# Windowed attention of an odd layer as one plan over 64 head groups, TensorE in source order

## The chip, the cores and the metric

The kernel runs on one core of a Trainium2 chip. The metric is the device time of one execution in microseconds. The five engines run side by side, each with its own queue in order: TensorE (PE; its weight loads are shown as PEld), VectorE (DVE), ScalarE (ACT), GpSimd (POOL) and SyncE (SP), which here only issues DMAs.

## The reference

Two layers over 2048 latent tokens of width 1024, with 256 context tokens beside them. The even layer (Fourier mixing beside latent attention with 8 heads) is not touched by the change. The odd layer is

```python
q, k, v, g = split_cols(h_lat @ w_in, ODD_SPLITS)      # 16 q heads, 4 kv heads, head width 64
ck, cv = split_cols(h_ctx @ w_in[:, GQA_Q:GQA_Q + 2 * GQA_KV], (GQA_KV, GQA_KV))
s_ctx  = einsum('bnqhgd,bchd->bnhgqc', qb, kc) * GQA_SCALE        # 256 context tokens
s_band = einsum('bnqhgd,bnkhd->bnhgqk', qb, kb) * GQA_SCALE       # 3 blocks of 128 tokens
s_band = where(abs(qpos - kpos) <= 128 and 0 <= kpos < n, s_band, -inf)
p = softmax(concatenate([s_ctx, s_band, s_sink], axis=-1))        # a sink logit per head
y_l = (windowed_gqa(q, k, v, ck, cv, sink_hg) * silu(g)) @ w_out
x = x + g_l * y_l;  out = rmsnorm(x, final_g)
```

All is in f32 with split operands: a number is a rounded high part plus the rest, and a product of two such is three matmuls.

## The kernel before

The last stage of the kernel works on 16 blocks of 128 query tokens. A block has four head groups (kv = 0 to 3), each of four q heads that share one k and v head. A group has 5 key tiles of 128 (two of context, three of the band; 4 in the first and the last block). So there are 64 groups and 312 steps; one step is one key tile of one group.

`step6` (L1809) does a step. On PE it computes the scores, transposed (keys by 4 x 128 queries), into a PSUM bank: a mask matmul at the band's two ends (L1813), the high parts' product with q's two halves stacked over 128 rows (L1814), and k's low part (L1815), whose extra rows carry the negated row maximum, so that the exponent's shift comes with the matmul. ACT takes the exponential twice, to f32 (L1819) and to f16 (L1820). The difference of the two is the low part `pl`; L1821 lets POOL compute it, and DVE in two of a block's twenty steps. The products with v (PV) are put in a list `pvq` and run four steps later: three f16 matmuls for each of four heads (L1831 to L1833, 65, 64 and 65 columns), which sum high and low parts of v into the same columns. They accumulate over a group's steps in one of two PSUM banks (`ppv`). At a group's end DVE divides by the sum plus the sink term (L1837 to L1840), and POOL multiplies by the gate (L1842).

The maximum of a query's scores is needed before its first step. So a block ahead, for each of 16 heads, the plain scores are computed again: `max_band` (L1525, reduced by DVE in L1529) and, two heads at a time, `max_ctx` (L1538, L1541). `chain` (L1545) combines the maxima of all 16 heads of the next block with small DVE operations, and `aug` (L1564) transposes them for a group on PE (L1566) and writes them under q's high part (L1567). `load_q6` (L1502) loads a group's q from DRAM by three DMAs, into one of six slots; `prep_k` (L1475) loads a key tile.

The output of the block before is woven in: `out_load` (x from DRAM), `out_tr` (eight PE transposes, L1868, split by ACT and DVE), `out_mm` (48 matmuls at L186 to L188, with one PSUM bank, `ppo`, for everything) and `out_fin` (L1885): the square sum on ACT, the power on POOL (L191), the multiply by scale and gain on DVE (L1894), and the store by SP. The output weights are loaded and split (`wload`, `wsplit`) during block 0.

For each block a plan is made: a list of (position in the block from 0 to 1, function), from the tables in `TP`. After every step the functions due by then are emitted, then PV down to four waiting ones; what is left of the plan comes at the block's end, `out_fin` last (0.999). SP's DMAs are held to the order of emission (L150). PE's instructions are not, in this stage: the scheduler that builds the program may exchange them. In the even layer's attention (main function `step`, matmuls at L155, L1188 on POOL) PE is held to the order of emission, tiles go by pairs, and PV is two matmuls a head with 129 and 65 columns.

Before this stage, the odd layer's projections run in 15 passes (n = 0 to 14); the lists `e6` are emitted between the matmuls of passes 11 to 14 and hold constants, the first key tiles, block 0's q, all maxima of block 0, its chain and the first `aug`.

## Time and profile before

| | us |
|---|---|
| median of 3 runs (lowest, highest) | 3039.12 (3033.49, 3039.51) |
| the profiled execution | 3034.24 |
| its span, first to last instruction | 3032.2 |
| PE busy in the span | 2861.0 |
| POOL, DVE, ACT busy | 1632.0, 1462.6, 1427.4 |
| mean granted clock of PE | 0.983 |

Busy time of PE is from the starts of its matmuls to modelled ends, so it is not PE at its peak. A view of waits names who ended an engine's idle time. A view of groups gives, for each line and shape, the count, the busy time, the mean of one and the idle time before. A timeline gives each instruction's start and length. DVE, ACT, POOL, PE and SP stand for the engines named above; sbf, sbr and sby are SBUF, psb is PSUM, q1h and q1l are q's two parts in DRAM.

### The profile page before, as it was taken

How to read it: one execution, taken by the hardware profiler on the slowest of the kernel's cores; microseconds unless marked ns; L12 is line 12 of the kernel's file. 1: busy time of each engine (PE TensorE's matmuls, PEld its weight loads, DVE VectorE, ACT ScalarE, POOL GpSimd, SP SyncE). 2: the span in 40 equal slices, each digit the busy share in tenths (PEclk: the TensorE clock that was granted, in tenths of full speed). 3: DMA queues.
4: the chain of work that ended last, by engine and by line, in shares of the span. 5: the costliest groups of instructions: out<-in, count | busy, mean ns of one | idle time of the engine just before them, and what ended most of it. 6: DMA issues, size and time to landing. Idle time of an engine off the chain costs nothing. (4 is left out here: it accounts for less than half of the span.)

```text
span 3032.2 us, 54284 instructions
## 1 busy us (share of the span) xinstructions
PE 2861.0 (94%) x21388; PEld 2299.7 (76%) x21388; DVE 1462.6 (48%) x2884; ACT 1427.4 (47%) x2131; POOL 1632.0 (54%) x1221
## 2 busy tenths in 40 slices
PE   7999999999999999999999998999997899999998
PEld 4787777877777777777777888989786666677666
DVE  3323315453656665666542234323234666676664
ACT  4333213223577777777773332232222645554554
POOL 2202204035588888888784434353443766766665
PEclk9999999999999999999999998999998999999999
DMA  6453335466310111011016545544464333223321
GB/s 240 153 177 134 130 122 173 142 213 223 104 44 26 44 40 44 26 44 40 26 35 232 188 153 177 187 141 162 152 189 156 105 105 98 84 77 93 102 83 45
DMA packets 299399, 357.13 MB, mean 118 GB/s; under 512 B 40884, under 2 KB 210172, under 8 KB 299144
## 3 DMA queue, kind: packets, MB, share of 16 engines
q1 hardware_dynamic: 231320, 258.73, 27.0%
q10 hardware_dynamic: 67824, 94.93, 8.9%
q8 instruction: 168, 2.75, 0.4%
q14 instruction: 87, 0.71, 0.1%
HBM read 245.82 MB, written 107.76 MB: 117 GB/s over the span
## 5 line engine op out<-in xcount | busy, mean ns | idle before, releaser
L186 PE MATMUL psb<-sbr 128*128 128x512 f32 (+3 forms) x2054 | 744.3, 363 | 14.4 <-ACT sbf L1022 5.7
L188 PE MATMUL psb<-sbr 128*128 128x512 f32 (+3 forms) x2054 | 722.9, 352 | 4.8 <-DVE sbr L183 4.8
L187 PE MATMUL psb<-sbr 128*128 128x512 f32 (+3 forms) x2054 | 723.8, 352 | 2.2 <-POOL sbr L183 2.2
L1188 POOL TENSOR_TENSOR sbf<-sbf 128x1024 f16<-128x1024 f32 (+1 forms) x296 | 624.2, 2112 | 140.8 <-ACT sbf L1187 76.9
L155 PE MATMUL psb<-sbr 100*128 100x512 f32 (+1 forms) x2408 | 624.2, 399 | 21.0 <-DVE sbr L955 14.4
L155 PEld LDWEIGHTS psb<-sbr 100*128 100x128 f32 (+1 forms) x2408 | 425.0, 190 | 112.8 <-issue 17.3
L942 DVE TENSOR_REDUCE sbf<-psb 128x1 f32<-128x512 f32 (+1 forms) x584 | 400.7, 690 | 218.1 <-PE psb L155 203.5
L186 PEld LDWEIGHTS psb<-sbr 128*128 128x128 f32 (+1 forms) x2054 | 390.7, 190 | 81.0 <-issue 12.3
L188 PEld LDWEIGHTS psb<-sbr 128*128 128x128 f32 (+1 forms) x2054 | 390.2, 190 | 63.9 <-DVE sbr L183 6.8
L187 PEld LDWEIGHTS psb<-sbr 128*128 128x128 f32 (+1 forms) x2054 | 390.8, 190 | 53.2 <-POOL sbr L183 3.9
L1821 POOL TENSOR_TENSOR sbf<-sbf 128x512 f16<-128x512 f32 x282 | 338.0, 1213 | 116.0 <-issue 60.1
L1186 ACT ACTIVATE sbf<-psb 128x1024 f32<-128x1024 f32 (+1 forms) x296 | 299.6, 1012 | 200.4 <-PE psb L155 180.5
L183 DVE TENSOR_TENSOR sbr<-sbf,sbr 128x512 fp32r<-128x512 f32 (+3 forms) x212 | 209.1, 1014 | 382.2 <-ACT sbr L180 381.1
L180 ACT CAST sbr<-sbf 128x512 fp32r<-128x512 f32 (+4 forms) x286 | 198.2, 731 | 394.5 <-PE psb L187 149.5
L183 POOL TENSOR_TENSOR sbr<-sbf,sbr 128x512 fp32r<-128x512 f32 (+4 forms) x113 | 166.1, 1482 | 367.9 <-ACT sbr L180 226.3
L1819 ACT ACTIVATE sbf<-psb 128x512 f32<-128x512 f32 x312 | 188.4, 604 | 282.1 <-PE psb L1815 249.8
L1187 ACT ACTIVATE sbf<-psb 128x1024 f16<-128x1024 f32 (+1 forms) x296 | 297.8, 1006 | 0.0
L155 PEld LDWEIGHTS <-sbf 128*128 128x128 f16 x4672 | 213.5, 97 | 72.9 <-issue 65.9
L155 PE MATMUL psb<-sbf 128*128 128x129 f16 (+1 forms) x4672 | 256.8, 207 | 5.2 <-DVE sbf L1214 2.9
L1529 DVE CUSTOM_DVE_ANT_0 sbf<-psb,sbf 128x384 bf16<-128x384 f32 (+1 forms) x256 | 137.8, 538 | 119.4 <-PE psb L1525 108.1
L1820 ACT ACTIVATE sbf<-psb 128x512 f16<-128x512 f32 x312 | 188.2, 603 | 5.5 <-DMA vd<-sbf 5.5
L1831 PEld LDWEIGHTS <-sbf 128*128 128x128 f16 x1248 | 115.5, 97 | 68.3 <-issue 61.8
(259 smaller groups left out, 4303.9 us busy)
## 6 DMA issues: line engine op xcount, KB each, us to landing
sbf<-in_o_w_in_t SPq DMA_DIRECT2D x60, 512.0 KB
sbf<-in_w_in_t SPq DMA_DIRECT2D x54, 512.0 KB
sbf<-in_x SPq DMA_DIRECT2D x32, 512.0 KB
sbf<-in_w_mod SPq DMA_DIRECT2D x32, 512.0 KB
sbr<-q1h SPq DMA_DIRECT2D x128, 128.0 KB
h1d<-sbf ACTq DMA_DIRECT2D x9, 1024.0 KB
sbf<-h1d SPq DMA_DIRECT2D x18, 512.0 KB
x1d<-sbf ACTq DMA_DIRECT2D x16, 512.0 KB
```

The lines of the kernel that those rows point to most:

```text
L155: tc.keep_in_program_order(nc.tensor.matmul(*args, **kw))
L180: act.copy(hi, src)
L183: e_lo.tensor_sub(lo, src, hi)
L186: pe.matmul(ps, sh, mh, start=start, stop=False)
L187: pe.matmul(ps, sh, ml, start=False, stop=False)
L188: pe.matmul(ps, sl, mh, start=False, stop=stop)
L942: dve.reduce_max(st["mx"][:, js[0] : js[-1] + 1, c], ps[:, 0 : len(js) * kn].rearrange("p (j k) -> p j k", k=kn), axis=AX.X)
L1186: act.activation(pf[:, :, 0:n], ps[:, :, 0:n], AF.Exp, scale=MLA_SCALE)
L1187: act.activation(ph[:, :, 0:n], ps[:, :, 0:n], AF.Exp, scale=MLA_SCALE)
L1188: pool.tensor_sub(pl[:, :, 0:n], pf[:, :, 0:n], ph[:, :, 0:n])
L1819: act.activation(pf, ps, AF.Exp, scale=GQA_SCALE)
L1821: (dve if (TP["b0"].get("sub", TP["sub"]) if b == 0 else TP["sub"])[kv][n] else pool).tensor_sub(pl, pf, ph)
```

## The change

The stage gets one plan for all 312 steps instead of one for each block, with positions counted in steps.

- PE is held to the order of emission in this stage too.
- Maxima, chain, sink and augment go by groups: a group's maxima lie 9 to 5 steps ahead of its first step, its chain (a DVE reduction over three values, a negation on ACT, an addition on POOL, the sink's exponential on ACT) right behind, its `aug` 2.2 steps ahead. The negated maximum is one rounded row set of 4, no longer a high and a low one (72 rows become 68).
- A group's q is loaded five groups ahead.
- Steps go by pairs: the f32 and f16 exponentials lie in two-tile buffers, and POOL subtracts 1024 columns at once. DVE subtracts only in the last group.
- PV is two matmuls a head with 129 and 65 columns; a group's sums take two PSUM banks, in one buffer instead of two. PV runs after every second step, down to six waiting ones; a group's last PV is moved ahead of the next step where it is first in the list.
- At a group's end DVE adds the low part by four scalar-tensor operations. The multiply by the final gain goes from DVE to POOL, the scaling of the output row to ACT.
- The two transposes of the output stand 3.2 steps apart, its matmuls 0.95 steps each, and `out_fin` follows 25 steps after the end of its own block.
- Block 0's maxima of the third and fourth group move out of the stage before; q and key tiles for block 0 are loaded a pass earlier there.

```diff
@@ tables of positions @@
-    'b0': {'mx': [0.1, 0.41, 0.59, 0.68], 'mcd': [0.1, 0.26, 0.08, 0.13]},
-    'pps': 3,
-    'ppv': 2,
-    'ppo': 1,
-    'ppx': 2,
-    'sub': [[0, 0, 0, 0, 1], [0, 0, 0, 0, 0], [0, 0, 1, 0, 0], [0, 0, 0, 0, 0]],
-    'lag': 4,
...
@@ const6 @@
+        C6["mask4"] = c6.tile([4, 4, P], F32, name="mask4b")
+        sp.dma_start(C6["mask4"], A["c_mask8"][0:4])
+        for u in range(8):
+            C6["mx", u] = c6.tile([P, 4, 3], F32, name=f"mx6{u}")
+            act.copy(C6["mx", u][:, :, 2], sk8[:, u % 4 * 4 : u % 4 * 4 + 4])
...
@@ maxima, chain, sink, augment @@
-            op0=ALU.add, op1=ALU.max, accum_out=mx[:, 0, 4 * kv + j : 4 * kv + j + 1],
+            op0=ALU.add, op1=ALU.max, accum_out=mx[:, j, 0:1],
-    def chain(b):
-        mx = MX.pop(b)
-        sk8 = C6["sk8"]
-        m = sm6.tile([P, 16], F32, tag="m", name=f"m6_{b}")
-        dve.tensor_max(m, mx[:, 0, :], mx[:, 1, :])
-        dve.tensor_max(m, m, sk8)
-        dve.tensor_scalar(m, m, -1.0, SHIFT / GQA_SCALE, op0=ALU.mult, op1=ALU.add)
-        m8 = M8[b] = sm6.tile([P, 4, 2, 4], F32, tag="m8", name=f"m86_{b}")
-        m4 = m.rearrange("p (k j) -> p k j", k=4)
-        dve.tensor_copy(m8[:, :, 0, :].bitcast(F32R), m4)
-        dve.tensor_sub(m8[:, :, 1, :].bitcast(F32R), m4, m8[:, :, 0, :])
-        es = ES[b] = sm6.tile([P, 16], F32, tag="es", name=f"es6_{b}")
-        pool.tensor_add(es, m, sk8)
-        if b:
-            sink(b)
-    def sink(b):
-        act.activation(ES[b], ES[b], AF.Exp, scale=GQA_SCALE)
+    def chain(b, kv):
+        m = sm6.tile([P, 4], F32, tag="m", name=f"m6_{b}_{kv}")
+        dve.reduce_max(m, C6["mx", 4 * (b % 2) + kv], axis=AX.X)
+        v = VM[b, kv] = sm6.tile([P, 4], F32, tag="vm", name=f"vm6_{b}_{kv}", bufs=3)
+        act.activation(v.bitcast(F32R), m, AF.Copy, bias=SHIFT / GQA_SCALE, scale=-1.0)
+        es = ES[b, kv] = sm6.tile([P, 4], F32, tag="es", name=f"es6_{b}_{kv}", bufs=4)
+        pool.tensor_add(es, v, C6["sk8"][:, 4 * kv : 4 * kv + 4])
+    def sink(b, kv):
+        act.activation(ES[b, kv], ES[b, kv], AF.Exp, scale=GQA_SCALE)

     def aug(b, kv):
         ps = ppx.tile([P, 512], F32, tag="x", name=f"xa{b}_{kv}")
-        pe.transpose(ps[0:8, 0:P], M8[b][:, kv].rearrange("p a j -> p (a j)"), ident)
+        pe.transpose(ps[0:4, 0:P], VM[b, kv], ident)
         dve.tensor_mul(
-            Q2[b, kv][64:72, :].rearrange("p (j t) -> p j t", t=P),
-            ps[0:8, None, 0:P].to_broadcast([8, 4, P]), C6["mask8"],
+            Q2[b, kv][64:68, :].rearrange("p (j t) -> p j t", t=P),
+            ps[0:4, None, 0:P].to_broadcast([4, 4, P]), C6["mask4"],
...
@@ steps laid into the last passes of the stage before @@
-        [const6, nop, *pk[0], nop, *pk[1], nop, *pk[2]],
-        [*pk[3], nop, *pk[4]],
-        [lambda: load_q6(0, 0)] + [nop] * 5 + max_all(0),
-        [lambda kv=kv: load_q6(0, kv) for kv in range(1, 4)] + [nop] * 3 + max_all(1) + max_all(2) + max_all(3)
-        + [lambda: chain(0)] + [nop] * 3 + [lambda: aug(0, 0)],
+        [const6, nop, *pk[0], nop, *pk[1], nop, *pk[2], nop, *pk[3]],
+        [nop] * 4 + [lambda: load_q6(0, 0)] + [nop] * 4,
+        [nop] * 4 + max_all(0) + [lambda: chain(0, 0)],
+        [lambda: load_q6(0, 1), lambda: load_q6(0, 2), *pk[4]] + [nop] * 4 + max_all(1) + [lambda: chain(0, 1), nop]
+        + [lambda: aug(0, 0)],
...
@@ step6 @@
-    pps, ppv, ppo = psum(TP['pps']), psum(TP['ppv']), psum(TP['ppo'])
+    pe = pe_ordered
+    pps, ppv, ppo = psum(3), psum(1), psum(1)
     O, G = {}, {}
     pvq = []
-    def step6(b, kv, n, t, nk):
+    PF = {}
+    def step6(b, kv, n, t, nk, x):
         side = None if t < 2 else 0 if t == 2 + b - 1 else (1 if t == 2 + b + 1 else None)
         ps = pps.tile([P, 512], F32, tag="s", name=f"s6_{b}_{kv}_{t}")
         if side is not None:
             pe.matmul(ps, C6['idb'], C6['mskb'][:, side], start=True, stop=False)
         pe.matmul(ps, kslice(kv, t), Q1[b, kv], start=side is None, stop=False)
         pe.matmul(ps, KL[t][:, kv, :], Q2[b, kv], start=False, stop=True)
-        pf = pp6.tile([P, 512], F32, tag="pf", name=f"pf6_{b}_{kv}_{t}", bufs=TP["pf"])
-        ph = pp6.tile([P, 512], F16, tag="ph", name=f"ph6_{b}_{kv}_{t}")
-        pl = pp6.tile([P, 512], F16, tag="pl", name=f"pl6_{b}_{kv}_{t}")
-        act.activation(pf, ps, AF.Exp, scale=GQA_SCALE)
+        if not x:
+            PF["f"] = pp6.tile([P, 2, 512], F32, tag="pf", name=f"pf6_{b}_{kv}_{t}", bufs=2)
+            PF["h"] = pp6.tile([P, 2, 512], F16, tag="ph", name=f"ph6_{b}_{kv}_{t}")
+            PF["l"] = pp6.tile([P, 2, 512], F16, tag="pl", name=f"pl6_{b}_{kv}_{t}")
+        pf, ph, pl = PF["f"], PF["h"][:, x], PF["l"][:, x]
+        act.activation(pf[:, x], ps, AF.Exp, scale=GQA_SCALE)
         act.activation(ph, ps, AF.Exp, scale=GQA_SCALE)
-        (dve if (TP["b0"].get("sub", TP["sub"]) if b == 0 else TP["sub"])[kv][n] else pool).tensor_sub(pl, pf, ph)
+        if b == 15 and kv == 3 and n > 1:
+            (pool if x else dve).tensor_sub(pl, pf[:, x], ph)
+        elif x:
+            pool.tensor_sub(PF["l"], pf, PF["h"])

         def pv():
             last = n == nk - 1
             v = V1[t]
             if n == 0:
-                O[b, kv] = ppv.tile([P, 512], F32, tag="o", name=f"o6_{b}_{kv}")
+                O[b, kv] = ppv.tile([P, 1024], F32, tag="o", name=f"o6_{b}_{kv}")
             for j in range(4):
-                o = O[b, kv][:, j * P : j * P + 65]
+                o = O[b, kv][:, j * 256 : j * 256 + 129]
                 js = slice(j * P, (j + 1) * P)
-                pe.matmul(o, ph[:, js], v[:, kv, 0:65], start=n == 0 and j == 0, stop=False)
-                pe.matmul(o[:, 0:64], ph[:, js], v[:, kv, 65:129], start=False, stop=False)
-                pe.matmul(o, pl[:, js], v[:, kv, 0:65], start=False, stop=last and j == 3)
+                if j % 2 and n:
+                    pe.matmul(o[:, 0:65], pl[:, js], v[:, kv, 0:65], start=False, stop=False)
+                    pe.matmul(o, ph[:, js], v[:, kv, 0:129], start=False, stop=last)
+                else:
+                    pe.matmul(o, ph[:, js], v[:, kv, 0:129], start=n == 0 and j % 2 == 0, stop=False)
+                    pe.matmul(o[:, 0:65], pl[:, js], v[:, kv, 0:65], start=False, stop=last and j % 2 == 1)
             if last:
                 p4 = O.pop((b, kv)).rearrange("p (j t) -> p j t", j=4)
                 den = sm6.tile([P, 4, 1], F32, tag="den", name=f"den{b}_{kv}")
-                dve.tensor_add(den, p4[:, :, 64:65], ES[b][:, 4 * kv : 4 * kv + 4, None])
+                dve.tensor_add(den, p4[:, :, 64:65], ES[b, kv][:, :, None])
                 dve.reciprocal(den, den)
                 t1 = sm6.tile([P, 4, 64], F32, tag="t1", name=f"t16_{b}_{kv}")
                 dve.tensor_mul(t1, p4[:, :, 0:64], den.to_broadcast([P, 4, 64]))
+                for j in range(4):
+                    dve.scalar_tensor_tensor(t1[:, j], p4[:, j, 65:129], den[:, j], t1[:, j], op0=ALU.mult, op1=ALU.add)
                 g = G[b][:, kv * 256 : kv * 256 + 256].rearrange("p (j d) -> p j d", j=4)
-                (dve if b == 15 and kv == 3 else pool).tensor_mul(g, g, t1)
-        pvq.append(pv)
+                pool.tensor_mul(g, g, t1)
+        pvq.append((pv, n == nk - 1))
...
@@ output @@
-            (pool if TP['e_xa'][hf] else dve).tensor_add(x[:, hsl], x[:, hsl], t)
+            pool.tensor_add(x[:, hsl], x[:, hsl], t)
-        dve.tensor_scalar(v, ss, 1.0 / D, EPS, op0=ALU.mult, op1=ALU.add)
+        act.activation(v, ss, AF.Copy, bias=EPS, scale=1.0 / D)
         rsqrt(y, v)
-        dve.scalar_tensor_tensor(x, x, y, C6["fgb"], op0=ALU.mult, op1=ALU.mult)
+        pool.tensor_mul(x, x, C6["fgb"])
+        act.mul(x, x, y)
...
@@ the plan (in place of the loop over blocks with a plan for each) @@
+    def tiles_of(b):
+        lo, hi = band(b)
+        return [0, 1] + [2 + i for i in range(lo, hi + 1)]
+    nts = [len(tiles_of(b)) for b in range(16)]
+    S = [4 * sum(nts[:b]) for b in range(17)]
+    groups = [(b, kv) for b in range(16) for kv in range(4)]
+    start = [S[b] + kv * nts[b] for b, kv in groups]
+    plan = []
+    def at(pos, f):
+        plan.append((pos, len(plan), f))
+    def g_load(b):
         G[b] = yp6.tile([P, D], F32, tag="g", name=f"g6_{b}", bufs=2)
         sp.dma_start(G[b], g1d[b])
+    at(-1, lambda: (sink(0, 0), sink(0, 1)))
+    for u, (b, kv) in enumerate(groups):
+        if u > 2:
+            at(start[u - 5] + 0.3 if u > 5 else -1, lambda b=b, kv=kv: load_q6(b, kv))
+        if u > 1:
+            s0 = start[u] - 9
+            for j in range(4):
+                at(s0 + 0.8 * j, lambda b=b, kv=kv, j=j: max_band(b, kv, j))
+            for jj in range(2):
+                at(s0 + 3.2 + 0.8 * jj, lambda b=b, kv=kv, jj=jj: max_ctx(b, kv, jj))
+            at(s0 + 4.1, lambda b=b, kv=kv: (chain(b, kv), sink(b, kv)))
+        if u:
+            at(start[u] - 2.2, lambda b=b, kv=kv: aug(b, kv))
+    for x in range(TP["wa"], 17):
+        w0 = S[0] + 1.5 * (x - TP["wa"]) if x > TP["wa"] else -1
+        if x < 16:
+            at(w0, lambda x=x: wload(*wl_[x]))
+        if x > TP["wa"]:
+            at(w0, lambda x=x: wsplit(*wl_[x - 1]))
+    at(S[1], out_const)
+    for b in range(16):
+        at(S[b] - 0.5, lambda b=b: g_load(b))
+        if b < 13:
+            at(S[b] + 6.6, lambda b=b: [f() for f in prep_k(b + 5)])
         if b == 15:
+            break
+        s1 = S[b + 1]
+        t0, t1, m0, md = (5, 8.2, 9.3, 0.95) if b < 13 else (5, 8.2, 9.3, 0.65) if b == 13 else (3, 6, 6.5, 0.42)
+        at(s1 + t0, lambda b=b: out_tr(b, 0))
+        at(s1 + t1, lambda b=b: out_tr(b, 1))
+        at(s1 + m0, lambda b=b: out_load(b))
+        for i in range(16):
+            at(s1 + m0 + md * i, lambda b=b, i=i: out_mm(b, i // 8, i % 8))
+        at(s1 + m0 + md * 16 + 0.6, lambda b=b: out_fin(b))
+    at(S[15] + 14, lambda: out_load(15))
+    at(S[15] + 13.4, lambda: tail_tr(0, 0, 4))
+    for i in range(8):
+        at(S[15] + 15 + 0.1 * i, lambda i=i: tail_mm(i // 2, i % 2))
+    plan.sort(key=lambda z: z[:2])
+    def run(pos):
+        while plan and plan[0][0] < pos:
+            plan.pop(0)[2]()
+    def run_pv(keep):
+        while len(pvq) > keep:
+            pvq.pop(0)[0]()
+    run(0)
+    g = 0
+    for b in range(16):
         for kv in range(4):
+            for n, t in enumerate(tiles_of(b)):
+                if g % 2 == 0 and pvq and pvq[0][1]:
+                    pvq.pop(0)[0]()
+                step6(b, kv, n, t, nts[b], g % 2)
+                g += 1
+                run(min(g - 0.5, S[15] + 14.9))
+                if g % 2 == 0:
+                    run_pv(6 if b < 15 else 4)
+                    run(min(g, S[15] + 14.9))
+    tail_tr(1, 4, 2)
+    run(S[15] + 15.45)
+    run_pv(2)
+    run(S[16])
+    tail_mm(4, 0)
+    run_pv(0)
+    tail_mm(4, 1)
+    tail_mm(5, 0)
+    tail_mm(5, 1)
+    tail_tr(2, 6, 2)
     tail_end()
```

## Rows read from the trace of the kernel before

**Rows 1.** The page: busy time of each engine, share of the span, and instructions.
```profile
PE 2861.0 (94%) x21388; PEld 2299.7 (76%) x21388; DVE 1462.6 (48%) x2884; ACT 1427.4 (47%) x2131; POOL 1632.0 (54%) x1221
```

**Rows 2.** Sums by stretch (us); columns: stretch, length, busy us of each engine, clock, DMA.
```profile
850.00:1440.00 590.00, 574.12 (x5206) 453.85 (x5205) 365.83 (x710) 431.44 (x471) 487.21 (x247) 1.00 0.14 39
2280.00:2335.00 55.00, 44.09 (x331) 43.53 (x330) 28.22 (x68) 11.09 (x19) 20.67 (x21) 0.88 0.47 150
2335.00:2377.10 42.10, 27.94 (x215) 19.24 (x213) 19.48 (x48) 23.49 (x45) 30.83 (x29) 0.72 0.43 133
2377.10:2976.20 599.10, 554.59 (x5326) 416.23 (x5325) 400.06 (x978) 324.65 (x633) 394.66 (x367) 0.99 0.31 90
2637.80:2680.10 42.30, 39.24 (x384) 29.20 (x381) 28.51 (x69) 23.07 (x46) 28.05 (x26) 1.00 0.31 94
2976.20:3032.20 56.00, 44.80 (x398) 32.90 (x394) 19.02 (x40) 23.30 (x46) 31.58 (x29) 0.96 0.16 57
```

**Rows 3.** Waits, blocks 1 to 14: who waited for whom, us, times, longest.
```profile
PE psb L1525 <- DMA sbr<-q1l: 14.9, 9, 2.2
...
PE psb L1566 <- DVE sbf L1555: 11.5, 15, 1.1
...
PE psb L1868 <- DVE sby L183: 8.7, 13, 0.7
...
PE psb L1525 <- DMA sbr<-q1h: 5.3, 4, 1.9
```

**Rows 4.** Waits of the DMA queue SP, blocks 1 to 14.
```profile
SPq L150 <- DVE sbf L1894: 332.3, 13, 25.6
```

**Rows 5.** Timeline of PE in a block's middle: start us, length, what.
```profile
2664.77 0.20 PE L1831 MATMUL psb<-sbf 128*128 128x65 f16 x1
...
2665.14 0.48 PE L1814 MATMUL psb<-sbr 128*128 128x512 f32 x1
2665.46 0.40 PE L1815 MATMUL psb<-sbr 72*128 72x512 f32 x1
2665.69 0.40 PE L1538 MATMUL psb<-sbr 128*128 128x256 f32 x2
```

**Rows 6.** Timeline of PE in the even layer's attention.
```profile
1004.69 0.87 PE L155 MATMUL psb<-sbf 128*128 128x129 f16 x16
1005.36 0.94 PE L155 MATMUL psb<-sbr 100*128 100x512 f32 x3
```

**Rows 7.** Groups by shape, even layer's attention: busy us, mean ns, idle before.
```profile
L1188 POOL TENSOR_TENSOR sbf<-sbf 128x1024 f16<-128x1024 f32 x211 | 450.8, 2138 | 103.5 <-ACT sbf L1187 54.7 <-PE psb L155 35.6 <-PE psb L159 7.4
...
L1214 DVE SCALAR_TENSOR_TENSOR sbf<-psb,sbf 128x64 f32<-128x64 f32 x106 | 22.8, 275 | 0.0
```

**Rows 8.** Groups by shape, blocks 1 to 14 of the odd layer.
```profile
L1821 POOL TENSOR_TENSOR sbf<-sbf 128x512 f16<-128x512 f32 x253 | 302.8, 1212 | 99.6 <-issue 50.2 <-ACT sbf L1820 30.8 <-POOL sbf L1821 12.1
...
L1883 POOL TENSOR_TENSOR sbf<-sbf 128x512 f32<-128x512 f32 x28 | 35.9, 1282 | 0.5
L1821 DVE TENSOR_TENSOR sbf<-sbf 128x512 f16<-128x512 f32 x28 | 31.8, 1135 | 9.9 <-ACT sbf L1820 9.0 <-POOL sbf L1883 0.9
...
L1889 ACT ACTIVATE sbf<-sbf 128x1024 bf16<-128x1024 f32 x14 | 14.8, 1058 | 0.0
```

**Rows 9.** Timeline of POOL at a block's start.
```profile
2640.21 5.51 POOL L1821 TENSOR_TENSOR sbf<-sbf 128x512 f16<-128x512 f32 x4
...
2658.11 0.73 POOL L1842 TENSOR_TENSOR sbf<-sbf 128x256 f32<-128x256 f32 x1 [5.69 <-DVE sbf L1840]
```

**Rows 10.** Timeline of DVE, at a block's start and in its middle.
```profile
2640.26 2.18 DVE L1894 SCALAR_TENSOR_TENSOR sbf<-sbf 128x1024 f32<-128x1024 f32 x1 [1.57 <-POOL sbf L191]
...
2643.19 0.16 DVE L1837 TENSOR_TENSOR sbf<-psb,sbf 128x4 f32<-128x4 f32 x1
...
2643.60 0.42 DVE L1840 TENSOR_TENSOR sbf<-psb,sbf 128x256 f32<-128x256 f32 x1
...
2665.08 0.69 DVE L1821 TENSOR_TENSOR sbf<-sbf 128x512 f16<-128x512 f32 x1 [0.17 <-ACT sbf L1820]
```

More of the change, by code (lines that the diff above doesn't have):

```diff
@@ L1446, in tile_hybrid @@
     LAG6 = 3
[L1447 removed]
+    c6, qp6, qs6, sm6, pp6, yp6 = sbuf(), sbuf(), sbuf(), sbuf(2), sbuf(5), sbuf()
     wr6 = sbuf(2)
@@ L1519, in max_band @@
         m0 = 0 if b else P
-        if b not in MX:
-            MX[b] = sm6.tile([P, 2, 16], F32, tag="mx", name=f"mx6_{b}")
-        mx = MX[b]
+        mx = C6["mx", 4 * (b % 2) + kv]
         s = lo % RING
@@ L1900, in tail_tr @@
     def tail_tr(q, k0, n):
+        if not q:
+            YT[15] = (
+                yp6.tile([P, KT, P], F32R, tag="yh", name="yh6_15"),
+                yp6.tile([P, KT, P], F32R, tag="yl", name="yl6_15"),
+            )
         yh, yl = YT[15]
```

138 lines of the change are left out of this document (13 added, 125 removed).

## The prediction

> **What bounds the kernel now.** I read the page first. TensorE (PE) is busy 94% of the span, no other engine above 54% [rows 1], so only PE's time counts, and in it two things: what PE streams and where it stands still. Then the sums by stretch [rows 2]. The changed code runs from about 2335 us to the end: block 0 takes 42.1 us, blocks 1 to 14 together 599.1 us (42.8 each), block 15 with the tail 56.0 us. In the 599.1 us PE is busy 554.6, idle 44.5 (7.4%). The even layer's attention does the same kind of work by pairs of tiles, and there PE is idle 15.9 of 590.0 us (2.7%). Ends of matmuls are modelled, so short waits hide inside "busy"; the true idle time is somewhat larger in both.
>
> What PE waits for in blocks 1 to 14 is in the waits [rows 3]: 20.2 us for q tiles coming from DRAM (14.9 + 5.3), 11.5 us for the max chain of 16 heads before the first augment transpose of a block, 8.7 us for the single PSUM bank between the two output transposes. That makes 40.4 of the 44.5 us, and all three sit at block ends, where the old plan has bunched its dependent steps. Why the q tiles are late is told by the DMA queue's own waits [rows 4]: SP sits 332.3 us, in 13 waits of up to 25.6 us, on VectorE's last multiply of the output (L1894). The output store is issued by SP in program order, and the loads of the next block's q stand behind it.
>
> The start is worse per microsecond: in block 0 PE is busy 27.9 of 42.1 us, at a mean granted clock of 0.72, and in the 55 us before it 44.1, at 0.88 [rows 2]. The new plan's first loads bear on that too.
>
> **The change part by part.**
>
> *The plan over 64 groups.* Loads of q move from the block's start to five groups ahead (a group is 5 steps, a step now 42.8/20 = 2.14 us); first use comes 16 steps, some 34 us, after the issue, against 4 steps before. The output store still blocks SP, but now at a place where everything behind it has such a lead; a store that waits even 25.6 us [rows 4] would leave 8. So the 20.2 us go. The chain of 16 heads becomes a small one per group, with the transpose 2.7 steps behind the last max (before: 0.4 steps): the 11.5 us go. The two output transposes stand 3.2 steps apart instead of back to back: the 8.7 us go. Bound below: none goes, if the same DMAs come late for another reason: 0. Above: 40.4 us. What is late next are the short releases that every plan has, and for their size I take the nearest pattern, the even layer's 2.7% idle.
>
> *TensorE work.* The twelve PV matmuls of a tile (65, 64, 65 columns for four heads) become eight (129, 65). Twelve take 0.37 us (2664.77 to 2665.14 [rows 5]); sixteen of the even layer's, two tiles' worth, take 0.67 us (1004.69 to 1005.36 [rows 6]), 0.335 a tile. Saved 0.035 x 280 = 10 us in blocks 1 to 14. The first f32 matmul after f16 ones takes 0.32 us to the next, where one behind f32 takes 0.23 [rows 5]: 0.09 us per switch. With steps in pairs there is one switch per pair; 140 x 0.09 = 12.6 us at most, 0 at least, since masks and side work stand at different places; I take 7. Mask, score, max, output matmuls and transposes keep their shapes (72 rows against 68, and 8 columns against 4, leave the streamed columns as they are): 0. Pinning the order removes departures such as a max matmul between two PV matmuls of one tile, worth a switch of 0.09 us each, and takes away the freedom to run ahead of a late input; I count both at 0, and the second is what rival 2 lives on.
>
> Sum for blocks 1 to 14: busy 554.6 - 10 - 7 = 538, and with 2.7% idle 538/0.973 = 553; 599 - 553 = 46 us less. The lower clock in that stretch (mean 0.99 [rows 2], 1% of 599 us) goes with the waits before it: 5 us more. Together 51, or 39.1 us a block.
>
> *Subtractions by pairs, on GpSimd alone.* Ten pairs a block at 2.14 us [rows 7] are 21.4 us; before, 253 singles at 1.21 in 14 blocks are 21.9 a block, beside two on VectorE at 1.14 [rows 8]. GpSimd further gets the multiply by the final gain (two halves of 1.28 [rows 8], 2.6 us) and four additions for one (at most 0.7 us). Its 28.1 us of a 42.3 us block [rows 2] become about 31 of 39, 79%, against 487/590 = 83% in the even layer, where that load goes with 2.7% idle of PE. Cost: 0 while PE covers it.
>
> *ScalarE.* Seven more small instructions a block (0.2 us each as an estimate, VectorE's nearest being 0.16 [rows 10], and at most 0.6) and the scaling of the output row (nearest: the square over 1024, 1.06 us [rows 8]): 23.1 [rows 2] becomes about 26 of 39 us, at most 28. Cost 0 as busy time; its waits are a rival below.
>
> *VectorE.* Loses L1894 (2.18 us a block [rows 10]), two subtractions (2.3) and the chain (some 2, an estimate from ten-odd small instructions a block at 0.16 and up); gains four small PSUM multiplies per group, nearest the even layer's 0.275 us each [rows 7], 16 x 0.275 = 4.4 us, and four reductions (0.2 each). 28.5 us of 42.3 [rows 2] become some 27 of 39. What leaves are the SBUF-only operations, and those slow GpSimd: four subtractions beside L1894 take 5.51 us (1.38 each), and the stretch's mean is 1.21 [rows 8 to 10]. That is worth GpSimd's slack, not PE's time.
>
> *The accumulator in PSUM.* Two single banks become one pair of banks in one buffer. So the first PV of a group waits until the last of the group before has been read: 0.83 (2643.19 to 2644.02 [rows 10]) + 4 x 0.275 [rows 7] = 1.9 us on VectorE. Behind the waiting matmul stands everything, since PE is in order. The cover is two steps' scores and side work, two steps of 1.95 us less their PV: about 3.2 us. Cost between 0 and, with two VectorE instructions of 0.7 us in front, 0.1 us x 64 = 6; I take 0 here, since the even layer has the same single pair of banks within its 2.7%.
>
> *Block 0 and the stage before.* Block 0 now loads its q tiles three groups deep before anything waits, and computes only groups 2 to 5's maxima beside its own steps. GpSimd sets its length: 8 pairs x 2.14 + 10 weight splits x about 1.3 (nearest: 1.28 for the same size [rows 8]) + 4 x 0.73 [rows 9] = 33 us, with ramp 36: 6 us less (bounds 0 and 14, the idle time of rows 2). In the stage before, 12 of the 24 maxima matmul groups leave the last pass, and q and k loads move up one pass: of 10.9 us idle there [rows 2] I take 5 (bounds -5, if the earlier loads collide, and 11).
>
> *The tail.* Four PSUM multiplies more after the last PV (1.1 us) and a GpSimd multiply (0.73 [rows 9]) for a VectorE one (0.42, as L1840 [rows 10]): +1.4 us. Block 15's own waits: 0 to -5; I take -2.
>
> Sum against the profiled execution (3034.2 us, of which 2.0 lie outside the span): -51 - 6 - 5 + 1.4 - 2 = -63, so 2971 us. The median of the runs, 3039.1, lies 4.9 above that execution; I give it about half of this: **2973 us**. The likeliest case's own range comes from 1% and 5% idle in blocks 1 to 14 (10 us less, 13 more) and the bounds of block 0, the stage before and the switches: 2945 to 3000.
>
> **The rivals.**
> 1. *ScalarE or GpSimd takes over as the bound.* ScalarE is in order, and each group now puts two waits in its queue: the negated max waits for VectorE's reduction, the sink for GpSimd's addition, which stands behind a pair of 2.14 us; the output scaling waits for GpSimd's 2.6 us multiply. With 2.5 us held per group and 3 for the output: 26 + 10 + 3 = 39 us, already PE's length, and queueing makes it 41. Against: three score banks and a lag of six PV steps take up holds of that length. Then 14 x (42.8 - 41) = 25 us are won there, with block 0 and the rest 37: 2999 us. GpSimd alone at the contended 1.38 us per 512 would be 10 x 2.76 + 9.6 = 37 a block, the same region.
> The Trainium skill ("GPSIMD Engine Reference", 4.1 Engine selection) speaks against this part: elementwise work on a tile belongs on VectorE, since GpSimd takes about twice as long for two inputs. By that rule the 30 subtractions and 15 multiplies moved make GpSimd late, which is this rival and its 2999 us. The trace has 1.21 against 0.69 us where VectorE is left alone [rows 8, 10], so the ratio holds, but the load stays below PE's.
> 2. *Slower: the single accumulator.* If VectorE's queue puts the group's readout late, PE stands at every one of 64 group boundaries, with all later matmuls behind it. It decides from 63/64 = 1.0 us per boundary; at 2 us (five VectorE instructions of 0.7 us in front of the readout: 3.5 + 1.9 - 3.2 = 2.2) it is +128 - 63 = +65: about 3100 us. For it: VectorE is 27/39 busy and in order, and the old kernel had two buffers. Against: the even layer.
> 3. *No change*: the plan only moves the waits, each of the three reappearing elsewhere, about 3039 us. Against: SP's 332.3 us have one cause, and it is moved away from.
>
> **How the numbers follow.** Forecast 0.58, rival 1 0.22, rival 2 0.13, rival 3 0.04; the rest, 0.03, is a gain beyond 2945. Within 0.2% (6 us; what a measurement of this kernel can tell) I put 0.05; faster 0.81 (forecast, most of rival 1, the rest); slower 0.14. The range 2940 to 3045 leaves out most of rival 2 and a little below.
>
> **What would show it.** Right: SP's long wait on the output is still there, but PE no longer waits for q; PE idle in the middle blocks under 4%, a block near 39 us; the PV pair at 0.33 us; GpSimd pairs at 2.1 to 2.2 us. Wrong: PE waiting on the readout of the accumulator at group ends (rival 2), or ScalarE's exponentials waiting on GpSimd while PE waits on ScalarE (rival 1).

## The result and the profile after

The changed kernel takes 3068.27 us (median of 4 runs, 3066.83 to 3073.39) against 3036.30 for the kernel before, run beside it: ratio 1.011, 95% interval 1.0089 to 1.013. It is about 32 us (1.1%) slower; 2973 was forecast, and the time lies above the range.

First the sums by stretch of the kernel after (columns as in [rows 2]: stretch, length, busy us and instructions of PE, PEld, DVE, ACT and POOL, the granted clock, the DMA engines' share and GB/s). In order they are the stage before, block 0, blocks 1 to 13, one middle block, block 14, block 15, the rest.

```profile
2280.00:2331.00 51.00, 39.86 (x304) 38.44 (x305) 22.77 (x51) 12.50 (x24) 24.68 (x26) 0.88 0.45 142
2331.00:2366.30 35.30, 22.08 (x142) 17.60 (x142) 14.99 (x50) 21.59 (x47) 25.30 (x19) 0.69 0.50 151
2366.30:2943.20 576.90, 515.48 (x3873) 403.65 (x3897) 335.69 (x1043) 323.37 (x702) 393.16 (x288) 0.92 0.31 89
2632.70:2677.00 44.30, 39.78 (x301) 31.14 (x302) 25.76 (x81) 25.02 (x55) 30.09 (x23) 0.92 0.32 92
2943.20:2993.30 50.10, 45.25 (x346) 35.40 (x348) 29.25 (x97) 26.22 (x58) 31.63 (x25) 0.93 0.16 49
2993.30:3035.70 42.40, 32.38 (x214) 24.57 (x214) 13.90 (x43) 20.38 (x45) 24.34 (x18) 0.83 0.07 26
3035.70:3066.90 31.20, 15.59 (x84) 11.67 (x84) 9.55 (x24) 5.11 (x11) 8.35 (x8) 0.77 0.14 50
```

Block 0 and the stage before came out as forecast: together 86.3 us, where the terms give 86.1 (36.1 + 50). The border between the two is the first exponential here and the first score matmul in [rows 2], so the sum is the better comparison. A middle block takes 44.4 us, where 42.8 was before and 39.1 forecast; PE is idle 61.4 of 576.9 us (10.6%), and the mean granted clock is 0.92 where it was 0.99. Blocks 14, 15 and the rest together take 123.7 us.

What PE waits for in blocks 1 to 13 is in the waits (who waited for whom, us, times, longest), to be set beside [rows 3]:

```profile
PE psb L128 <- POOL sbf L1817: 30.0, 13, 2.6
PE psb L124 <- DVE sby L152: 14.2, 13, 1.2
PE psb L124 <- DVE sbf L1815: 11.5, 12, 1.0
```

q is gone from the list, and so is the old chain. SP's own long wait is still there, 313.3 us from block 0 to the end for the output's scaling (answering to [rows 4]), and PE no longer waits for any DMA:

```profile
SPq L119 <- ACT sbf L1871: 313.3, 15, 38.1
```

In their place stands above all one wait per block for the gate multiply on POOL (L1817). The timeline of a block's start shows it. PE first:

```profile
2646.64 0.38 PE L128 MATMUL psb<-sbf 128*128 128x128 f32 x2
2649.39 0.50 PE L128 MATMUL psb<-sbf 128*128 128x128 f32 x2 [2.37 <-POOL sbf L1817]
2649.59 0.63 PE L124 MATMUL psb<-sbr 128*128 128x384 f32 x1
2650.01 0.65 PE L124 MATMUL psb<-sbf 128*128 128x512 bf16 x1
2653.02 1.65 PE L124 MATMUL psb<-sbr,sby 128*128 128x512 f32 x3 [1.08 <-DVE sby L152]
```

and, in the same microseconds, the last input of the gate multiply on VectorE and POOL's queue:

```profile
2644.39 0.86 DVE L1815 SCALAR_TENSOR_TENSOR sbf<-psb,sbf 128x64 f32<-128x64 f32 x4
```

```profile
2643.53 2.14 POOL L1791 TENSOR_TENSOR sbf<-sbf 128x1024 f16<-128x1024 f32 x1
2645.62 0.20 POOL L1522 TENSOR_TENSOR sbf<-sbf 128x4 f32<-128x4 f32 x1
2645.77 2.36 POOL L1870 TENSOR_TENSOR sbf<-sbf 128x1024 f32<-128x1024 f32 x1
2648.09 0.55 POOL L160 TENSOR_TENSOR sbf<-sbf 128x1 f32<-128x1 f32 x1
2648.61 0.72 POOL L1817 TENSOR_TENSOR sbf<-sbf 128x256 f32<-128x256 f32 x1
```

Of the second four output transposes, two run at 2646.64 and the other two need the heads of the block's last group, whose gate multiply POOL begins at 2648.61. VectorE had finished its input at 2645.25; in between POOL ran the new multiply by the final gain (L1870, 2.36 us) of the block before and its rsqrt (L160, 0.55). PE is in source order, so a row-maximum matmul of a later group (the 128x384) and the next step's scores behind it stand still behind two transposes.

The second cost of the wait shows in three stretches of that block, cut at the wait (columns as above):

```profile
2632.70:2646.60 13.90, 12.82 (x105) 9.98 (x105) 10.26 (x33) 8.81 (x22) 9.58 (x9) 1.00 0.03 8
2646.60:2649.40 2.80, 0.43 (x4) 0.15 (x2) 0.91 (x3) 1.25 (x3) 2.73 (x3) 1.00 0.03 9
2649.60:2656.40 6.80, 5.72 (x35) 4.34 (x34) 1.86 (x4) 3.63 (x8) 4.26 (x2) 0.50 0.71 211
```

PE stands for 2.4 us, and right behind that the clock is at the lower level (1.2 of 2.4 GHz) for 6.8 us. The bf16 mask matmul, 0.39 us at full clock, takes 0.65. The 5.72 us of work in that stretch would be about 2.9 at full clock. So, as an estimate, the wait of 2.4 us costs some 5 here. The price is not the same everywhere: e2 below has stops of the same length with 3.4 us at the lower clock behind them.

### The profile page after: what moved, and what is told of

Its sections match the earlier page's. It is cut to its first block, busy times and chain, and to the rows that moved or that the text cites. A ratio compares the mean times of both kernels' runs of the same rounds, so it can differ in the third digit from the quotient of the medians.

```text
span 3066.9 us, 52010 instructions
## 1 busy us (share of the span) xinstructions
PE 2863.1 (93%) x20110; PEld 2324.0 (76%) x20140; DVE 1421.7 (46%) x3064; ACT 1457.4 (48%) x2281; POOL 1665.0 (54%) x1159
## 5 line engine op out<-in xcount | busy, mean ns | idle before, releaser
L124 PE MATMUL psb<-sbr 96*128 96x512 f32 (+6 forms) x3492 | 945.8, 402 | 28.1 <-DVE sbr L924 14.4
L124 PEld LDWEIGHTS psb<-sbr 96*128 96x128 f32 (+3 forms) x3492 | 633.8, 195 | 173.0 <-issue 29.5
L124 PE MATMUL psb<-sbf 128*128 128x129 f16 (+1 forms) x7258 | 453.3, 214 | 35.5 <-DVE sbf L1815 16.8
L124 PEld LDWEIGHTS <-sbf 128*128 128x128 f16 (+1 forms) x7288 | 357.1, 100 | 150.2 <-issue 128.1
L1791 POOL TENSOR_TENSOR sbf<-sbf 128x1024 f16<-128x1024 f32 x155 | 331.9, 2142 | 176.1 <-issue 69.0
L149 ACT CAST sbr<-sbf 128x512 fp32r<-128x512 f32 (+4 forms) x286 | 198.4, 731 | 388.9 <-PE psb L156 152.3
L124 PE MATMUL psb<-sbr,sby 128*128 128x512 f32 (+1 forms) x740 | 237.6, 427 | 16.4 <-DVE sby L152 16.0
```

Of the source, the lines that this page charges most:

```text
L124: tc.keep_in_program_order(nc.tensor.matmul(*args, **kw))
L1791: pool.tensor_sub(PF["l"], pf, PF["h"])
```

## The experiments

Times are medians. The kernel before was run beside them on the same chip (3036.5 us for e1 to e4, 3035.5 for e5 to e8, 3035.1 for e9 to e12), and each ratio is against it. "A block" is the time between the first exponentials of two blocks, read from the timeline of ScalarE. Line numbers are those of the changed kernel, except that without the pin they are one lower from L1768 on, e8 has those of the kernel before, and the readout of e10 has its own.

**e1, the output's finish three steps later.**

```diff
-        at(s1 + m0 + md * 16 + 0.6, lambda b=b: out_fin(b))
+        at(s1 + m0 + md * 16 + (3.6 if b < 14 else 0.6), lambda b=b: out_fin(b))
```

> Only the output's finish (square sum, GpSimd multiply by the gain and power, ScalarE scaling) is emitted 3 steps later, for blocks 0 to 13. Theory A (the moved gain multiply): in the changed kernel PE stands 2.4 us a block at the second output transpose, waiting for the gate multiply of the block's last head group, which stands in GpSimd's queue behind the 2.36 us gain multiply and the 0.55 us power; then the clock is at its lower level for 6.8 us a block. Without them in front the gate is ready 2.9 us earlier: the wait goes, the clock stays up, a block goes from 44.4 to about 38.5 us, and the time from 3068 to about 2990. Theory B (the transpose is simply too early for the lag of PV, whatever stands in GpSimd's queue): part of the wait stays, over 1 us a block, the clock still falls: 3040 to 3068. Theory C (the single PSUM accumulator sets the pace): the wait goes, but PE waits as much at the group boundaries: 3050 to 3068.

3096.16 us, 1.0207 (1.0159 to 1.0255): slower than the kernel before, and 28 us slower than the changed one. PE's waits in the middle blocks:

```profile
PE psb L124 <- DVE sby L152: 46.5, 12, 4.4
PE psb L128 <- POOL sbf L1817: 23.5, 13, 1.9
```

The gate wait falls by 0.5 us a block only. That does not acquit the gain multiply, since the edit left it in front of the gate; POOL's queue at a block's start in this run:

```profile
2655.80 2.35 POOL L1870 TENSOR_TENSOR sbf<-sbf 128x1024 f32<-128x1024 f32 x1
2658.12 0.71 POOL L1817 TENSOR_TENSOR sbf<-sbf 128x256 f32<-128x256 f32 x1
```

Only the rsqrt (0.55 us) has moved behind the gate, and the wait fell by that much. So this run does not tell theory A from theory B. The rsqrt now also stands behind a pair of subtractions, the scaling on ACT waits for it (3.35 us there) ahead of ACT's part of the output split, and the first output matmul waits up to 4.4 us.

**e2, the second transposes 2.6 steps later** and the output matmuls behind them; the finish keeps its place.

```diff
-        t0, t1, m0, md = (5, 8.2, 9.3, 0.95) if b < 13 else (5, 8.2, 9.3, 0.65) if b == 13 else ...
+        t0, t1, m0, md = (5, 10.8, 11.8, 0.83) if b < 13 else (5, 10.8, 11.8, 0.65) if b == 13 else ...
...
-        at(s1 + m0 + md * 16 + 0.6, lambda b=b: out_fin(b))
+        at(s1 + (25.1 if b < 13 else m0 + md * 16 + 0.6), lambda b=b: out_fin(b))
```

> Only the second output transpose moves, from 8.2 to 10.8 steps behind its block, and the output matmuls behind it from 9.3 to 11.8 (0.83 steps each instead of 0.95); the output's finish stays at 25.1 steps. Theories A and B both say that PE no longer waits for the gate multiply and the clock stays up: a block near 38 to 39 us, about 2990 us, and somewhat less if the 1.4 us wait behind it (the first output matmul for VectorE's low part) goes too: 2975. Theory C: no gain worth naming, 3050 to 3068.

3057.28 us, 1.0068 (1.004 to 1.0095). The gate wait is gone from the middle blocks, and another of the same length has its place:

```profile
PE psb L124 <- DVE sby L152: 29.9, 13, 2.4
```

ACT's copy for the split (L149) now stands behind exponentials that the scaling's wait for POOL (L160, 1.55 us) has made late. The run also shows that the clock is part of a block's length: the stop of 2.41 us is followed by 3.4 us at the lower clock in most blocks, but not in block 5, which takes 42.8 us at a clock of 1.00, where block 6 takes 44.3 at 0.96 with the same idle time (4.56 us).

**e3, gain and scale back in one VectorE operation.**

```diff
-        pool.tensor_mul(x, x, C6["fgb"])
-        act.mul(x, x, y)
+        dve.scalar_tensor_tensor(x, x, y, C6["fgb"], op0=ALU.mult, op1=ALU.mult)
```

> Only the multiply by the final gain and the row scaling go back to VectorE as one instruction, as before the change. Theory A: the gate multiply is no longer behind 2.36 us on GpSimd, the wait goes from 2.4 to under 0.5 us, the clock stays up, about 2990 us; the 2.2 us on VectorE cost at most 0.5 us a block at the group readouts (2997). Theory B: the transpose still waits, 3040 to 3068. The Trainium skill's rule that two-input elementwise work is VectorE's would be borne out here by a mechanism of queue order.

3059.69 us, 1.008 (1.0038 to 1.0123). The wait for the gate is gone from the middle blocks but one (2.4 us in all). Again one wait for another; this is VectorE's queue and, behind it, PE:

```profile
2642.60 1.29 DVE L1870 SCALAR_TENSOR_TENSOR sbf<-sbf 128x1024 f32<-128x1024 f32 x1 [2.41 <-POOL sbf L160]
2643.80 0.47 DVE L1815 SCALAR_TENSOR_TENSOR sbf<-psb,sbf 128x64 f32<-128x64 f32 x2
```

```profile
2644.32 1.14 PE L124 MATMUL psb<-sbf 128*128 128x129 f16 x12 [3.75 <-DVE sbf L1815]
```

The multiply waits 2.41 us for POOL's rsqrt in the middle of the accumulator's readout, and the next group's PV waits for the readout's end.

**e4, PE not pinned in this stage**, all else as changed.

```diff
-    pe = pe_ordered
     pps, ppv, ppo = psum(3), psum(1), psum(1)
```

> Only the hold of TensorE to source order is taken off in this stage. If the pinned order is what turns a late gate into a wait of PE (theory D), the scheduler puts other matmuls ahead of the late transpose and the time falls by most of 13 x 5.9 us and of the tail's 8 us: 2990 to 3020. If the order that the scheduler makes is nearly the source's, or brings waits of its own, the time stays within 15 us of 3068.

3024.32 us, 0.9969 (0.9955 to 0.9983): 44 us less than the changed kernel, and 0.3% faster than before. PE's waits for the gate are 16.4 us in all and at most 1.4, against 30.0 and 2.6; the longest are now for exponentials:

```profile
PE psb L1777 <- ACT sbf L1786: 25.8, 13, 3.1
PE psb L1843 <- POOL sbf L1816: 16.4, 12, 1.4
```

**e5, the sink's exponential one step into its group** (meant to take it out of ACT's queue while POOL's addition is late).

```diff
-            at(s0 + 4.1, lambda b=b, kv=kv: (chain(b, kv), sink(b, kv)))
+            at(s0 + 4.1, lambda b=b, kv=kv: chain(b, kv))
+            at(start[u] + 1.1, lambda b=b, kv=kv: sink(b, kv))
```

> Only the sink's exponential is emitted 6 steps later (one step into its group, far ahead of its use at the group's end). In the changed kernel ScalarE stands 123.7 us in 60 waits on GpSimd's small addition in front of it. Theory E (ScalarE's holds make the score exponentials late, and through them GpSimd's pairs, the gate and the split of the transposes): the holds go, PE's waits of 2.5 and 1.4 us at a block's start shrink by half or more, and where the clock no longer falls a block goes to 39 to 41 us: 2985 to 3025. Theory B (positions of the transposes and first output matmuls against the chains they follow, whatever ScalarE does): the waits stay at over 1.5 us, 3050 to 3068.

3058.04 us, 1.0073 (1.0044 to 1.0102). The middle blocks stay at 44.4 us, and PE's gate wait is as before (29.3 us in 13). But the edit did not do what it was meant to do: in the same blocks ACT still stands 100.1 us on POOL's addition, in 40 waits, where the changed kernel has 110.0 in 51. So the 10 us gained say little about what ACT's holds cost.

**e6, three moves together**: e5's; transposes and output matmuls at (5, 9.8, 12.6, 0.78); the scaling and the store three steps behind the gain multiply, meant to spare ACT the wait for it.

```diff
         pool.tensor_mul(x, x, C6["fgb"])
+        FY[b] = x, y
+    def out_store(b):
+        x, y = FY.pop(b)
         act.mul(x, x, y)
...
+        at(f0 + (3 if b < 13 else 1.5 if b == 13 else 0.1), lambda b=b: out_store(b))
```

> Three edits together: the late sink, the second transpose at 9.8 steps with the output matmuls from 12.6 (0.78 steps each), and the output's scaling and store 3 steps behind its GpSimd part, so that ScalarE does not stand for it. If PE's waits at a block's start are all that keeps the plan from its sum (theories B and E), no wait over 1 us is left there, the clock stays at its upper level, a block is near 38.5 us and the time near 2985; the last two blocks and the tail keep what they lost, some 25 us. If a wait comes up elsewhere each time one is taken away (theory F: source order itself, at the present load of the other engines), a block stays over 42 us: 3035 or more.

3030.76 us, 0.9984 (0.9972 to 0.9996): 37 us less than the changed kernel, with PE still pinned. The third move did not shorten the wait it was meant for: from block 0 to the end ACT's scaling waits 28.3 us for POOL's rsqrt in 15 times, against 24.1 in 15 in the changed kernel. How the gain divides among the moves was not measured. The output matmuls now begin 2.8 steps behind the second transposes, where e2 had 1.0. PE's waits of over 2 us are gone from the middle blocks; what is left is rival 2's readout:

```profile
PE psb L124 <- DVE sbf L1815: 38.2, 28, 1.6
PE psb L128 <- POOL sbf L1817: 10.9, 13, 0.9
```

Blocks are 41.6 us in some cases and 43.2 in others. Two neighbours show the difference to be the clock: the same 300 matmuls keep PE busy 37.64 us at 1.00 and 39.25 at 0.96.

```profile
2404.90:2446.50 41.60, 37.64 (x300) 29.28 (x301) 25.55 (x81) 25.19 (x54) 30.23 (x22) 1.00 0.33 98
2446.50:2489.70 43.20, 39.25 (x300) 30.45 (x301) 25.61 (x81) 25.07 (x54) 30.22 (x22) 0.96 0.30 93
```

**e7, idle work in the waits**: the changed kernel with 12 matmuls that nobody reads before the second transposes and 6 before the first output matmul.

```diff
+        if b < 13:
+            at(s1 + t1, lambda b=b: dummy(b, 0, 12))
+            at(s1 + m0, lambda b=b: dummy(b, 1, 6))
```

> The changed kernel with work added: 12 bf16 matmuls of 512 columns (some 2.6 us) in front of the second output transpose and 6 (1.3 us) in front of the first output matmul, into a PSUM bank that nobody reads, for blocks 0 to 12. They fall into PE's waits. Theory G (a wait of PE costs twice: itself, and a stretch of 6.8 us at the lower clock behind it): the clock stays at its upper level there, a block loses about 3.4 us although it does more, and the time falls by up to 13 x 3.4 = 44 us, to 3025 to 3045. If the lower clock costs nothing (the engines behind PE set the pace in that stretch), the time stays within 8 us of 3068 or rises by what of the added 3.9 us a block does not fit the waits, up to 3090.

3049.81 us, 1.0042 (1.0022 to 1.0062): 18 us less than the changed kernel with 234 matmuls more. A block goes from 44.4 to 42.8 us; blocks 1 to 13 take 556.4 us (2369.1 to 2925.5), where they took 576.9. The same blocks and the first 13 us of block 14:

```profile
2369.10:2938.50 569.40, 542.44 (x4168) 409.02 (x4207) 344.12 (x1069) 331.78 (x719) 401.97 (x295) 1.00 0.31 91
```

The clock holds at 1.00 from block 2 to block 13. The lower clock behind the waits is what this takes away, and it is worth at least the 18 us; the added work, some 3.9 us a block by the expectation, takes part of it back where it outlasts the waits.

**e8, the kernel before with PE pinned in this stage.**

```diff
+    pe = pe_ordered
     pps, ppv, ppo = psum(TP['pps']), psum(TP['ppv']), psum(TP['ppo'])
```

> The kernel before with one part of the change alone: TensorE held to source order in the last stage. Theory D (source order turns late releases into waits of PE): slower than the kernel before, by 20 to 60 us (3056 to 3096), with PE waits at block ends over those 40 us that it had and a lower granted clock. If the order that the scheduler made was nearly the source's: within 8 us of 3036.

3155.3 us, 1.0394 (1.0363 to 1.0424): 120 us slower, twice the most that was expected. In blocks 1 to 14 PE is idle 132.4 of 712.0 us, where it was 44.5 of 599.1 [rows 2], at a mean clock of 0.90. The old plan's late q, up to 2.2 us of PE a time in [rows 3], now stops it for up to 8.3:

```profile
PE psb L155 <- DMA sbr<-q1l: 67.0, 9, 8.3
PE psb L155 <- DMA sbr<-q1h: 21.4, 3, 7.6
```

**e9, e6 without the pin** (the edits of e4 and e6).

> The three moved pieces of the run before (sink late, transposes and output matmuls spread, scaling three steps behind) with TensorE not pinned in this stage. Before here is about 3036 us; the pinned version of the same measured 3030.8, the changed kernel unpinned 3024.3, the changed kernel 3068.3. Theory P (a pinned queue turns each late input into a stop of TensorE; the order is only as good as its lateness): the pinned version still has 52 us of stops on the accumulator's readout and 25 us on the gate multiply, and free order fills half of them, so 2995 to 3015 us, with blocks of 39.5 to 41 us. Rival Q (the moved pieces and the free order cure the same waits, so the second cure adds nothing): 3020 to 3030 us, about the faster of the two alone.

3012.86 us, 0.9934 (0.9918 to 0.9949): 18 less than e6 and 11 less than e4. Both cures act, short of a sum; 2995 to 3015 was expected by the theory of lateness and order, and this lies at its upper end. A block is 41.1 us.

**e10, e6 with another readout.** The accumulator's two halves leave PSUM by a copy and an addition before anything is divided: three VectorE operations ahead of the release, not seven.

```diff
+                t1 = sm6.tile([P, 4, 64], F32, tag="t1", name=f"t16_{b}_{kv}")
+                dve.tensor_copy(t1, p4[:, :, 65:129])
+                dve.tensor_add(t1, t1, p4[:, :, 0:64])
                 dve.reciprocal(den, den)
-                t1 = sm6.tile([P, 4, 64], F32, tag="t1", name=f"t16_{b}_{kv}")
-                dve.tensor_mul(t1, p4[:, :, 0:64], den.to_broadcast([P, 4, 64]))
-                for j in range(4):
-                    dve.scalar_tensor_tensor(t1[:, j], p4[:, j, 65:129], den[:, j], t1[:, j], ...)
+                dve.tensor_mul(t1, t1, den.to_broadcast([P, 4, 64]))
```

> The same three moved pieces, pinned, and the accumulator's readout in another order: the two halves are copied and added out of PSUM first and divided afterwards in SBUF, so that three VectorE operations stand before the accumulator's release and not seven. Theory R (the single accumulator is now the limit of a pinned block: seven operations, with row maxima between them, hold the next group's first probability matmul for 1.7 us once a block and some 0.6 us three times): the 52 us of these stops fall to 15 to 25, blocks from 41.6 to 43.2 go to 40 to 41, and the time from 3030.8 to 3000 to 3012 us. Rival S (another input is late right behind: the gate multiply on GpSimd): under 8 us gained, 3023 to 3032, with the stops on the gate multiply above 35 us.

3013.03 us, 0.9929 (0.9916 to 0.9941): 18 us less than e6, one above the range expected (3000 to 3012). PE's waits on the readout fall from 38.2 to 9.1 us; next in line are the row maxima's banks (the readout is now L1813):

```profile
PE psb L124 <- DVE sbf L1499: 22.6, 14, 1.7
PE psb L124 <- DVE sbf L1813: 9.1, 20, 1.6
```

**e11, e10 with the end reordered.** In the changed kernel PE stands 8.1 us at the end of block 15, with ready output products behind it in the source:

```profile
3032.75 0.87 PE L124 MATMUL psb<-sbf 128*128 128x129 f16 x16
3041.72 0.69 PE L128 MATMUL psb<-sbf 128*128 128x128 f32 x2 [8.11 <-POOL sbf L1817]
3042.06 5.35 PE L124 MATMUL psb<-sbr,sby 128*128 128x512 f32 x15
```

ACT's queue says why the gate is late there: the scaling of block 14 waits for POOL, and the last exponential of the group stands behind it.

```profile
3038.13 1.15 ACT L1871 ACTIVATE sbf<-sbf 128x1024 f32<-128x1024 f32 x1 [1.86 <-POOL sbf L160]
3039.18 0.58 ACT L1787 ACTIVATE sbf<-psb 128x512 f16<-128x512 f32 x1
```

```diff
-    at(S[15] + 14, lambda: out_load(15))
+    at(S[15] + 15.7, lambda: out_load(15))
...
+    run(S[15] + 15.45)
     tail_tr(1, 4, 2)
-    run(S[15] + 15.45)
```

and `out_fin(14)` and its store at 15.5 and 15.6 steps into block 15.

> The run above, and at the end of block 15 two pieces in another order: the first eight output products of the last block are put ahead of the two transposes that wait 8 us for the gate multiply, and the finish of block 14 (square, gain, scaling, store) and the load behind it come after all score steps of block 15. If the 8.3 us stop with 15 ready matmuls (5 us) standing behind it is a matter of source order alone, 5 to 9 us less than the run above; if the gate multiply is late because the last exponentials are late, the stop only shrinks by the work pulled ahead and the end comes 2 to 5 us sooner; if the later finish of block 14 and the later load become the end, nothing or up to 4 us more.

3005.64 us, 0.9909 (0.9894 to 0.9924): 7.4 us less than e10, in the middle of what was expected of source order. Both edits have a part in it. The 15 matmuls, 5.35 us above, now run ahead of the gate; and the gate's transposes follow the start of the PV in front of them after 7.5 us, where the changed kernel and e10 have 9.0, so some 1.5 us come from the later finish. The longest gate wait at the end is 3.0 us now.

**e12, e11 without the pin.**

> All of the run above with TensorE not pinned in this stage. Theory P: 2985 to 3005 us, 5 to 20 us faster than the pinned version with the same edits. Rival (where no input is late, order in the source and free order give the same): within 5 us of the pinned version.

2982.83 us, 0.9837 (0.9822 to 0.9852): the fastest, 53 us below the kernel before and 85 below the changed one. 23 us less than e11, where the rival had "within 5". Blocks 1 to 14 and a little of block 15:

```profile
2364.00:2920.00 556.00, 528.44 (x4187) 409.91 (x4186) 395.11 (x1014) 353.52 (x762) 431.55 (x313) 0.98 0.33 97
```

Middle blocks take 39.3 us, some 40.2. PE is idle 27.6 of 556 us, 5.0%.

## Why the prediction was wrong

**The step that failed** is the term for the order: "Pinning the order … takes away the freedom to run ahead of a late input; I count both at 0". The loss was 44 us on this plan (e4), 120 on the old plan (e8), and still 18 and 23 once most inputs had been moved in time (e6 to e9, e11 to e12). The order cost was priced by the even layer, which is pinned with 2.7% idle; but what a pin cost here went by the late inputs on the plan, and the even layer has none of this stage's output work. The old plan's waits of [rows 3] were short because PE could run ahead: a wait for the same tiles is 2.2 us there at most, and 8.3 with the pin.

**What is late next** was the second half of the same error. "What is late next are the short releases that every plan has" had no name and no place. The gate multiply (L1817) is in the text as 0.73 us of POOL's work in block 0 and the tail, and never as something that PE waits for. It needs the last PV of a block, which runs up to six steps late, and stands in POOL's queue behind the gain multiply that the change puts there; that multiply was priced as busy time alone, "Cost: 0 while PE covers it". "The two output transposes stand 3.2 steps apart …: the 8.7 us go" was true of the bank and passed over this input.

By terms, a middle block against the 39.1 forecast: idle 4.7 us (61.4/13) instead of 1.1, +3.6; the stretch at half clock +2.9, which the forecast had as a gain of 0.4, so +3.3; PE's work with that stretch put at full clock 36.8 us (39.65 - 2.9) instead of 38.4, -1.6, which was not taken apart. Together +5.3, which is 44.4 - 39.1; over 13 blocks 69 us. Blocks 14, 15 and the rest take 123.7 us where the terms give 39.1 + 56.0 + 1.4 - 2 = 94.5: another 29, of which e11 shows 7.4, from the 8.1 us stop and the finish before it. Some of block 14's length is no loss: it carries 346 matmuls against 301, among them 24 more PV and 12 more for the output, since that of block 12 runs over into it. How the remainder divides was not measured.

**What held.** The q tiles, the chain and SP's wait went as described. Sixteen PV matmuls take 0.73 us (2663.00 to 2663.73 below) and elsewhere 0.67 (2666.71 to 2667.38), near the even layer's pair in [rows 6]; POOL's pairs take 2.14 us, as in [rows 7]. Block 0 and the stage before are within 1 us. And the length of a block was reachable: 39.3 us in e12, with the pairs and the single accumulator of the change, but without the pin, with another readout and with positions moved.

```profile
2663.00 0.87 PE L124 MATMUL psb<-sbf 128*128 128x129 f16 x16
2663.73 0.81 PE L124 MATMUL psb<-sbr 128*128 128x512 f32 x2
```

**The rivals.** Rival 2, the single accumulator, had the right mechanism: 1.0 us a block in the changed kernel, up to 3.75 us at a time in e3 and the first in line in e6. The text took 0 for it "since the even layer has the same"; e10 puts it at 18 us once the gate is out of the way, far from the 128 us priced. The even layer does not have the same: there the two banks are two buffers (`ppv`, psum(2)), and each is read by four VectorE operations and released by itself, where the change releases one buffer of two banks behind seven. Rival 1's holds are there as described, but PE hardly waits for exponentials in the middle blocks (0.3 us). They reach it by the output's split (e1, e2) and, at the end of block 15, by the gate (e11); in the middle block shown above the gate's input was there 3.4 us before POOL came to it. ACT's waits from block 0 to the end of the changed kernel:

```profile
ACT sbf L1525 <- POOL sbf L1522: 123.7, 60, 3.1
ACT sbf L1871 <- POOL sbf L160: 24.1, 15, 2.0
```

The Trainium skill ("GPSIMD Engine Reference", 4.1 Engine selection) would have the gain multiply on VectorE, and the durations agree with its factor of about two: 1.29 us on VectorE (e3, with the scale included) against 2.36 on GpSimd. Where GpSimd subtracts beside it they do not: there the same instruction took VectorE 2.18 us [rows 10]. The time does not follow either: e3 gains 9 us, and PE's longest wait, now on VectorE's queue, is 3.8 us instead of 2.6. Another sentence of the Trainium skill is the one to have used ("PSUM — Partial Sum Buffer", Engine vs sequencer instructions): "MATMULs start and complete in program order". The 8.1 us stop with 15 ready matmuls behind it agrees.

So far the cause is shown: taking off the pin, by one line, gives back 44 us (e4), and putting it on the old plan costs 120 (e8); the readout, again alone, gives 18 (e10); moved positions (e6) and the end's order (e11) give 37 and 7, each as a bundle. Together, without the pin, they give back 85 us (e12). ACT's holds were not taken away by themselves: e5 left most of them. That the gate is late in the middle blocks because of the gain multiply is read from POOL's queue, and e3, which takes it from there, has no such wait; no run took it away without another wait in its place. Why a block takes about 44.4 us in the changed kernel, e2, e3 and e5 alike, with different waits, was not explained.

## What to carry to other kernels

Before an engine is held to source order, list for each instruction that can wait the queue in front of its producer: with the pin, the latest input of any small side operation stops everything, and the price is the wait plus what the lower clock takes behind it. Moving one operation out of a queue can move the wait to the next queue of the chain: three moves at once gave 37 us, where single ones like them gave about 10 each, or lost 28. After an edit, look in the trace whether it took away what it was meant to: e1 left the gain multiply in front of the gate, and e5 left most of ACT's holds. The price of an order in one stage (2.7% idle in the even layer) need not hold in another with other side work.
